# A build-time scheduler that lets transfers queue for one shared bandwidth

## The chip, the cores and the metric

The kernel runs on one core of one Trainium2 chip. The metric is the device time of one execution in microseconds (us). A change of 0.2%, about 2.4 us, is roughly what a measurement of this kernel can tell from no change.

## What is computed

One layer of a hybrid decoder, on 1024 tokens of width 1024, in float32. The mixer has three groups of heads side by side: a short gated convolution (256 columns), a gated DeltaNet (512 columns, 4 heads of 128) and a stick-breaking attention (256 columns, 4 heads of 64).

```python
h = rmsnorm(x, w_norm_mix)
sc_b, sc_c, sc_h, gq, gk, gv, gz, ga, gb, sq, sk, sv = split(h @ w_mix_in)
y_sc = sc_b * causal_dwconv(sc_c * sc_h, w_sconv)
gq, gk, gv = split(silu(causal_dwconv([gq, gk, gv], w_gdn_conv)))
# DeltaNet, in chunks of 64 tokens: decay matrices from the gates,
# a triangular solve with (I + lower(k k^T)), then a scan over the chunks
o = gated_delta_rule_chunked(l2norm(gq), l2norm(gk), gv, g, beta)
y_gdn = rmsnorm(o, w_gdn_norm) * silu(gz)
y_sb = stick_breaking_attention(sq, sk, sv)
x = x + [y_sc, y_gdn, y_sb] @ w_mix_out
gate, val = split(causal_dwconv(rmsnorm(x, w_norm_ffn) @ w_ffn_up, w_ffn_conv))
x = x + (silu(gate) * val) @ w_ffn_down
return rmsnorm(x, w_norm_final)
```

## The kernel before

Every operand of a large product is split into a high and a low part, and a product is three matmuls (high by high, low by high, high by low), which are the lines L316, L318 and L320 for the in-projection and L1310, L1312 and L1314 for the out-projection.

The first half of the program, the *front* (the opening aside), is put in order by a small event simulator, the class `Flow`, that runs while the program is built. Each piece of work is a Python generator, a *process*. It yields a request: an engine with an estimated duration, a buffer to take, or an event to wait for. `Flow.grant` gives each engine to the request with the best class and due time among those that are ready in its model, advances the model's clock, and the process then emits its instructions. So the model's clock decides the order in which each engine's instructions stand in the program, for all five engines; on the chip each engine then runs its own list strictly in that order, and semaphores keep the data right. A model time that is too short or too long makes no wrong result; it puts instructions behind, or ahead of, others.

A transfer is issued on SyncE (SP). In `grant` it holds SP for 60 ns of model time, and the process that asked goes on after a landing time. `sp(kb)` makes it 2000 + 5 ns per KB: 3.28 us for 256 KB, 4.56 us for 512 KB. Each transfer has its landing time for itself, however many are under way. In `prep3` the first three of a block's four loads ask for a landing time of 0, and only the fourth, `sp(256)`, is waited for.

The processes that the prediction speaks of, and their names in the trace:
- `dense` (L537): the in-projection, a column tile `pd3` to `pd25` after the other, 8 steps each; one step is the three products of one pair of row blocks (two instructions each of L316, L318, L320). `pd22` and `pd23`, then `pd24` and `pd25` (which alternate), are the last. Their weights are `w22` and so on.
- `inverse` (L872): the triangular inverses of the DeltaNet chunks on VectorE. 31 pairs of operations on `iv` and `LL`, then three stream transposes (L902 once, L905 twice), which the chain's first products on TensorE, `pw1` and `pw0` (L949), need.
- `prep1`, `prep2`, `prep3`, `prep_at`, `prep_v`: for each of eight blocks of 128 tokens, loads of keys, queries, values and gates from DRAM (`ld<-kscr` and so on, 4 loads of 256 KB) and of a decay matrix (`m<-gscr`, 256 KB; the tile of block 0 is `m20`, of block 1 `m21`); then products on TensorE, `pk` (L1041), `pkq` (L1068), `pq` (L1077), `pv` (L1098), between exponentials on ScalarE (ACT) and elementwise work on VectorE (`kds`, `m`, `ld<-pv`).
- `chain` (L1106): the scan over the chunks with its products `pw`, `py`, `p`, `pco` (L1168) and `pyt` (L1196); the outputs go through DRAM (`yscr`) back to SBUF as `yr`, are split by ACT into `yh` and by VectorE into a low part.
- `mo_mm` (L1286): the out-projection `pmo0` to `pmo7`, with 8 weight tiles `wo0` to `wo7`; `wo0` and `wo1` take the columns that come from the short convolution (`a_sch`), `wo2` to `wo7` the others.

Behind the front the 22 pairs of up-projection column tiles and the down-projection are written out by hand.

Of the kernel before, what the change touches and what calls it, by code (L numbers as in the profile page):

```python
# [70 lines left out]
T_AFTER = dict(PE=230, DVE=60, ACT=60, POOL=60, SP=60)  # L71
T_PIPE = dict(PE=0, DVE=80, ACT=100, POOL=60, SP=0)
T_TABLE = 1280


class Flow:
# [4 lines left out]
    def __init__(self, **tokens):  # L81
        self.now = 0.0
        self.events, self.seq = [], 0
        self.free = dict.fromkeys(("PE", "DVE", "ACT", "POOL", "SP"), 0.0)
        self.want = {e: [] for e in self.free}
        self.tokens, self.queue = dict(tokens), {k: [] for k in tokens}
        self.happened, self.waiting = set(), {}
        self.port = dict(DVE=0.0, POOL=0.0)
        self.table = None

    def at(self, t, f, *args):
        self.seq += 1
        heapq.heappush(self.events, (t, self.seq, f, args))
# [64 lines left out]
    def grant(self, e):  # L158
        q = self.want[e]
        pick = heapq.heappop(q)  # L160
        if e == "ACT" and pick[3] not in (None, self.table):
            same = [r for r in q if r[3] in (None, self.table) and r[0] <= pick[0]]
            if same:
                q.append(pick)
                pick = min(same)
                q.remove(pick)
                heapq.heapify(q)
        _, _, ns, what, proc, cls = pick
        t = self.now
        if e == "ACT" and what not in (None, self.table):  # L170
            ns += T_TABLE
            self.table = what
        land = 0
        if e == "SP":
            ns, land = 60, ns
        elif e == "POOL" or e == "DVE" and what:
            other = "DVE" if e == "POOL" else "POOL"
            t = max(t, self.port[other])
            self.port[e] = t + ns
        self.free[e] = t + ns - T_PIPE[e]  # L180
        back, self.now = self.now, t + ns + land + (0 if what == "more" else T_AFTER[e])
        r = next(proc, None)
        if r is not None:
            self.at(self.now, self.handle, proc, cls, r)
        self.now = back
# [3 lines left out]
def trunk(ctx: ExitStack, tc: tile.TileContext, xT, x, cst, wcm, wsv, wout, wnf, wup, wdn, wfin, out):  # L189
# [24 lines left out]
    def e8(shape, name, dt=F32):  # L214
        return T(shape, dt, "e8", name)
# [7 lines left out]
    def small(shape, name, bufs=1):  # L223
        return T(shape, F32, name, name, bufs=bufs)
# [10 lines left out]
    def tt(eng, out_, a, b, op):  # L235
        eng.tensor_tensor(out_, a, b, op=op)  # L236
# [44 lines left out]
    def ms(name):  # L281
        return pp.tile([P, 512], F32, tag="ms", name=name, bufs=4)
# [105 lines left out]
    def pe(ns, due=None, what=None):  # L388

        return "PE", ns, due, what  # L390

    def act(n, table=None, cls=None):
        return "ACT", T_ACT[0] + T_ACT[1] * n, cls, table

    def dve(n, port=True, per=T_DVE, cls=None):
        return "DVE", per[0] + per[1] * n, cls, port

    def pool(n, cls=None):
        return "POOL", T_POOL[0] + T_POOL[1] * n, cls, None

    def sp(kb, cls=None):
        return "SP", 2000 + 5 * kb, cls, None

    def take(tag, n=1):
        return "take", tag, n

    def wait(*what):
        return "wait", what

    def now(*what):  # L410
        fl.happen(what)
# [385 lines left out]
    def load_blk(dst, scr, n):  # L797
        nc.sync.dma_start(dst, scr[:, :, n * P:(n + 1) * P].rearrange("h p c -> p h c"))

    def v4(t):  # L800
        return t[:, 0:512].rearrange("p (h c) -> p h c", h=GH)

    def load_gf(dst, n, m):

        nc.sync.dma_start(dst, gscr[n * GH:(n + m) * GH, :].rearrange("(o h) c -> o (h c)", o=1).broadcast_to([P, m * GH * P]))
# [5 lines left out]
    def bc(ap, m=P):  # L811
        return ap.unsqueeze(2).broadcast_to([P, GH, m])
# [180 lines left out]
    def prep3(n):  # L993
        s = st[n]
        if n == 0:
            for kind in ("gq", "gv", "gz"):
                for j in range(GH):
                    yield wait(kind, j)
            yield wait("norms", NB - 1)
            yield wait("sb", 1)  # L1000
            yield "ACT", 400, None, "exp"
            nc.scalar.preload_act_table_set("natural_log_exp_and_others")
            nc.scalar.activation(snk, nke, AF.Ln)
            nc.scalar.activation(snk, snk, AF.Exp, scale=0.5)
            nc.scalar.activation(egn, Gc, AF.Exp)
            yield "DVE", 200, None, True
            nc.vector.tensor_scalar(egn, egn, -1.0, None, op0=mul)
        else:
            yield wait("ld", n - 1)
        yield take("e8")  # L1010
        ld = e8([P, 4, GH, P], f"ld{n}")
        kb, qb, vb, zb = (ld[:, i] for i in range(4))
        for dst, scr in ((kb, kscr), (qb, qscr), (vb, vscr)):
            yield "SP", 0, None, None
            load_blk(dst, scr, n)
        yield sp(256)
        load_blk(zb, zscr, n)
        now("ld", n)
        if n > 0:
            yield wait("m2", n - 1)  # L1020
        yield take("e8")
        now("m2", n)
        yield sp(256)
        m2 = e8([P, 4, GH, P], f"m2{n}")
        at, dec, eg, kd = (m2[:, i] for i in range(4))
        load_gf(dec.rearrange("p h c -> p (h c)"), n, 1)
        s.update(kb=kb, qe=qb, kd=kd, vs=vb, at=at, zb=zb, jk=dec, m2=m2)
        now("dec", n)
        fl.spawn(prep_v(n), 3)
        fl.spawn(prep_at(n), 3)  # L1030
        yield act(512, "exp")
        nc.scalar.activation(eg, dec, AF.Exp)
        now("eg", n)
        yield pool(4)
        egl = s["egl"] = small([P, GH], "egl", bufs=3)
        nc.gpsimd.tensor_copy(egl, eg[:, :, P - 1])
        yield take("ms")
        yield pe(4 * 109)
        pk = ms(f"pk{n}")
        for h in range(GH):  # L1040
            nc.tensor.transpose(out=pk[:, h * P:(h + 1) * P], in_=kb[:, h, :], identity=ident)  # L1041
        yield wait("kds", n)
        yield dve(512, False)
        tt(nc.vector, kd, v4(pk), bc(s["kds"]), mul)
        fl.give("ms")
        now("kd", n)
# [45 lines left out]
    def prep_v(n):  # L1092
        s = st[n]
        yield take("ms")
        yield pe(4 * 109)
        pv = ms(f"pv{n}")
        for h in range(GH):
            nc.tensor.transpose(out=pv[:, h * P:(h + 1) * P], in_=s["vs"][:, h, :], identity=ident)  # L1098
        yield dve(512, False)
        tt(nc.vector, s["vs"], v4(pv), bc(snk[:, n, :]), mul)  # L1100
        fl.give("ms")
        now("v2", n)
# [993 lines left out]
```

## Time and profile before

| what | value |
|---|---|
| time, median of 3 runs | 1221.97 us (1221.42 to 1223.99) |
| the profiled execution | 1226.06 us, its span 1224.3 us |
| TensorE (PE) busy | 1191.8 us, 97% of the span |
| weight loads (PEld) | 992.8 us, beside the matmuls |
| VectorE (DVE) busy | 939.8 us, 77% |
| ScalarE (ACT) busy | 646.7 us, 53% |
| GpSimd (POOL) busy | 373.3 us, 30% |
| DMA | 152.76 MB, mean 125 GB/s |

The front ends at about 600 us. A row of a timeline gives the start in the span, the duration, the engine, the line, the operation with output and inputs, a count, and in brackets the idle time before it and what ended it. A row of a waits view gives what waited and for what: total us, times, longest. `PEclk` is the clock granted to TensorE, where 1.00 is the upper level.

### The profile page before, as it was taken

The page shows a single profiled execution, that of the slowest core. Times are in us where ns is not written, and L with a number is a line of the kernel's source. Part 1 is how long each engine was busy: PE and PEld are TensorE (multiplying, and loading weights), DVE is VectorE, ACT ScalarE, POOL GpSimd, SP SyncE. Part 2 cuts the span into 40 slices and gives each one's busy share as a digit, 9 for nine tenths or more (in the row PEclk, how much of TensorE's full clock was granted, in tenths as well). Part 3 has the DMA queues.
Part 4 walks back from the last instruction along what each step waited for, and adds up shares of the span by engine and source line. Part 5 has one row for each costly group of instructions (what it writes and reads, how often), then busy time and mean ns, then how long its engine had stood idle before and what let it go on. Part 6 is the DMA issues. An engine that isn't in the chain of part 4 may idle for free.

```text
span 1224.3 us, 16593 instructions
## 1 busy us (share of the span) xinstructions
PE 1191.8 (97%) x6083; PEld 992.8 (81%) x6083; DVE 939.8 (77%) x1340; ACT 646.7 (53%) x1102; POOL 373.3 (30%) x299
## 2 busy tenths in 40 slices
PE   8999999999999999999999999999999999999997
PEld 6798888888878878888788888888888887888886
DVE  3776779977993557557988988889889878985774
ACT  6766576778323544544655454553545534454554
POOL 3444433433335433000024544234443322001200
PEclk9999999999998989999999999999999999999999
DMA  9111132332271663444123333223333279852314
GB/s 347 53 56 43 54 127 89 106 108 91 87 217 36 178 169 102 140 142 141 60 67 99 128 112 111 82 97 115 116 108 104 69 267 352 300 138 81 99 52 146
DMA packets 87089, 152.76 MB, mean 125 GB/s; under 512 B 6592, under 2 KB 42464, under 8 KB 86752
## 3 DMA queue, kind: packets, MB, share of 16 engines
q1 hardware_dynamic: 86864, 151.59, 38.3%
q8 instruction: 48, 0.79, 0.3%
q14 instruction: 33, 0.27, 0.1%
q10 hardware_dynamic: 144, 0.10, 0.1%
HBM read 110.50 MB, written 41.17 MB: 124 GB/s over the span
## 4 chain that ended last, share of the span: by engine, by line
PE 81%; DVE 5%; DMA 5%; ACT 4%; issue 2%; SPq 1%; POOL 1%; ACTq 0%; DVEq 0%; POOLq 0%
PE pu L1571 19%; PE pz L1571 10%; PE pdx L1739 8%; PE pdzP L1739 7%; PE pd L316 6%; PE pd L318 5%; PE pd L320 5%; PE py L1571 4%; PE pmo L1310 2%; PE pmo L1312 2%; PE pmo L1314 2%; DMA m<-gscr 1%; PE po L690 1%; DMA xs<-x_in 1%; PE pa L668 1%
## 5 line engine op out<-in xcount | busy, mean ns | idle before, releaser
L236 POOL TENSOR_TENSOR ws<-wu 128x512 f32<-128x512 f32 x40 | 62.1, 1573 | 172.4 <-DMA wu<-wup_in 172.4
L236 POOL TENSOR_TENSOR sg<-sg,om 128x511 f32<-128x511 f32 (+3 forms) x64 | 60.7, 958 | 118.0 <-DVE om L653 62.1
L239 DVE SCALAR_TENSOR_TENSOR ua<-uv,ck,ua 128x1023 f32<-128x1023 f32 (+1 forms) x44 | 76.1, 1729 | 7.4 <-ACT ua L233 7.3
L239 DVE SCALAR_TENSOR_TENSOR ua<-ug,ck,ua 128x1023 f32<-128x1023 f32 (+1 forms) x44 | 76.0, 1727 | 0.8
L233 ACT ACTIVATE ua<-ug,ck 128x1024 f32<-128x1024 f32 x22 | 25.4, 1154 | 86.8 <-DVE ug L236 86.8
L1665 ACT ACTIVATE ua<-ua 128x1024 f32<-128x1024 f32 x22 | 23.4, 1062 | 84.8 <-DVE ua L239 84.8
L236 POOL TENSOR_TENSOR x<-x,wfb 128x512 f32<-128x512 f32 x8 | 12.8, 1636 | 126.3 <-ACT y L1755 126.3
L236 DVE TENSOR_TENSOR S<-ws,S 128x512 fp32r<-128x512 f32 x52 | 39.8, 770 | 5.5 <-ACT S L231 4.3
L236 DVE TENSOR_TENSOR at<-pa,at 128x512 fp32r<-128x512 f32 (+3 forms) x48 | 26.1, 549 | 22.6 <-ACT at L231 22.4
L231 ACT ACTIVATE S<-ws 128x512 fp32r<-128x512 f32 x52 | 32.5, 630 | 20.2 <-DVE ws L236 10.4
L1310 PE MATMUL pmo<-wo,yh 128*128 128x512 f32 x128 | 41.4, 404 | 0.0
L231 ACT ACTIVATE at<-pa 128x512 fp32r<-128x512 f32 (+3 forms) x48 | 23.4, 487 | 33.0 <-PE pa L668 31.7
L236 POOL TENSOR_TENSOR A<-wu,A 128x512 fp32r<-128x512 f32 x11 | 15.9, 1449 | 80.4 <-ACT A L231 80.4
L1312 PE MATMUL pmo<-wo,yh 128*128 128x512 f32 x128 | 39.7, 392 | 0.0
L1314 PE MATMUL pmo<-wo,yr 128*128 128x512 f32 x128 | 39.6, 390 | 0.0
L653 DVE TENSOR_TENSOR_SCAN om<-om 128x512 f32<-128x512 f32 (+3 forms) x32 | 33.7, 1066 | 7.0 <-ACT om L644 6.1
L236 DVE TENSOR_TENSOR A<-wu,A 128x512 fp32r<-128x512 f32 x29 | 28.4, 983 | 11.7 <-ACT A L231 11.7
L1571 PE MATMUL py<-fB21h,A 128*128 128x512 f32 x112 | 36.7, 389 | 0.0
L1571 PE MATMUL pz<-fB22h,S 128*128 128x512 f32 x112 | 36.7, 389 | 0.0
L1571 PE MATMUL pu<-fB11h,A 128*128 128x512 f32 x104 | 34.1, 389 | 0.0
L1571 PE MATMUL pu<-fT3h,S 128*128 128x512 f32 x104 | 34.1, 389 | 0.0
L1571 PE MATMUL pu<-fT4h,A 128*128 128x512 f32 x104 | 34.1, 389 | 0.0
(1446 smaller groups left out, 3958.9 us busy)
## 6 DMA issues: line engine op xcount, KB each, us to landing
wu<-wup_in SPq DMA_DIRECT2D x44, 512.0 KB, 3.9
gaP<-gst SPq DMA_DIRECT2D x77, 256.0 KB, 3.2
w<-wcm_in SPq DMA_DIRECT2D x23, 512.0 KB, 3.6
wd<-wdn_in SPq DMA_DIRECT2D x44, 256.0 KB, 5.9
gst<-g SPq DMA_DIRECT2D x12, 512.0 KB, 2.6
gst<-uv SPq DMA_DIRECT2D x10, 512.0 KB, 2.9
xs<-x_in SPq DMA_DIRECT2D x4, 1024.0 KB, 11.4
wor<-wout_in SPq DMA_DIRECT2D x8, 512.0 KB, 3.8
```

Of the source, the lines that this page charges most:

```text
L231: nc.scalar.activation(out_, in_, AF.Copy)
L236: eng.tensor_tensor(out_, a, b, op=op)
L239: nc.vector.scalar_tensor_tensor(out_, a, s, b, op0=op0, op1=op1)
L316: nc.tensor.matmul(ps[th], lhsT=w_h, rhs=xh[k // 2][:, k % 2, th * 512:(th + 1) * 512], start=first, stop=False)
L318: nc.tensor.matmul(ps[th], lhsT=w_h, rhs=xl[k // 2][:, k % 2, th * 512:(th + 1) * 512], start=False, stop=False)
L320: nc.tensor.matmul(ps[th], lhsT=w_l, rhs=xh[k // 2][:, k % 2, th * 512:(th + 1) * 512], start=False, stop=last)
L653: nc.vector.tensor_tensor_scan(om[:, 0:w][:, ::-1], om[:, 0:w][:, ::-1], om[:, 0:w][:, ::-1], init, op0=mul, op1=ALU.bypass)
L1310: nc.tensor.matmul(po[:, c * 512:(c + 1) * 512], lhsT=h, rhs=wh_[:, c * 512:(c + 1) * 512], start=first, stop=False)
L1312: nc.tensor.matmul(po[:, c * 512:(c + 1) * 512], lhsT=h, rhs=wl_[:, c * 512:(c + 1) * 512], start=False, stop=False)
L1314: nc.tensor.matmul(po[:, c * 512:(c + 1) * 512], lhsT=l, rhs=wh_[:, c * 512:(c + 1) * 512], start=False, stop=last)
L1571: nc.tensor.matmul(o, lhsT=w[:, wk], rhs=b[:, k, :], start=first and k + j == 0, stop=k == 3 and j == 2, skip_group_check=not first)
L1739: nc.tensor.matmul(o, lhsT=a[:, tk], rhs=b, start=first and u == 0 and j == 0, stop=u == NU - 1 and j == 2, skip_group_check=not first)
```

## The change

Three lines change the model. `grant` keeps one number, `moved`, the model time at which the transfers so far have been moved. A transfer of `what` KB adds 3.4 ns per KB to it, from the present time or from the end of the transfers ahead, whichever is later. Its process goes on 3 us (`T_LAND`) after that. So 256 KB alone take 3.87 us (before 3.28), 512 KB 4.74 (before 4.56), 64 KB 3.22 (before 2.32), and each transfer that is still queued ahead of one adds its own share, 0.87 us for 256 KB and 1.74 us for 512 KB. In `prep3` the first three loads of a block are not waited for, as before, but now count 256 KB each, so the fourth lands 2.6 us later, and what is issued behind them too.

```diff
--- before.py
+++ after.py
@@ -71,6 +71,8 @@
 T_AFTER = dict(PE=230, DVE=60, ACT=60, POOL=60, SP=60)
 T_PIPE = dict(PE=0, DVE=80, ACT=100, POOL=60, SP=0)
 T_TABLE = 1280
+T_KB = 3.4
+T_LAND = 3000
 
 
 class Flow:
@@ -87,6 +89,7 @@
         self.happened, self.waiting = set(), {}
         self.port = dict(DVE=0.0, POOL=0.0)
         self.table = None
+        self.moved = 0.0
 
     def at(self, t, f, *args):
         self.seq += 1
@@ -172,7 +175,9 @@
             self.table = what
         land = 0
         if e == "SP":
-            ns, land = 60, ns
+
+            self.moved = max(t, self.moved) + T_KB * what
+            ns, land = 60, ns and self.moved - t + ns
         elif e == "POOL" or e == "DVE" and what:
             other = "DVE" if e == "POOL" else "POOL"
             t = max(t, self.port[other])
@@ -399,7 +404,7 @@
         return "POOL", T_POOL[0] + T_POOL[1] * n, cls, None
 
     def sp(kb, cls=None):
-        return "SP", 2000 + 5 * kb, cls, None
+        return "SP", T_LAND, cls, kb
 
     def take(tag, n=1):
         return "take", tag, n
@@ -1011,7 +1016,7 @@
         ld = e8([P, 4, GH, P], f"ld{n}")
         kb, qb, vb, zb = (ld[:, i] for i in range(4))
         for dst, scr in ((kb, kscr), (qb, qscr), (vb, vscr)):
-            yield "SP", 0, None, None
+            yield "SP", 0, None, 256
             load_blk(dst, scr, n)
         yield sp(256)
         load_blk(zb, zscr, n)
```

No engine gains or loses an instruction, except that ACT loads its function tables 35 times where it did 42 times. The order within the front changes from about 225 us to the front's end on every engine; the hand-written part behind it stays nearly as it was. All lines shift by 2 to 5 (L902 is L907, L905 is L910, L949 is L954, L1168 is L1173, L1310 is L1315).

DVE at the end of the inverse, before:

```order
L236 TENSOR_TENSOR iv_2833<-LL_2082 128x60
L239 SCALAR_TENSOR_TENSOR m20_3163<-m20_3163,Gc_370,maskadd_74 128x128 x4
L236 TENSOR_TENSOR LL_2082<-LL_2082,iv_2833 128x2x30
L236 TENSOR_TENSOR ld0_3126<-pv0_3201,snk_374 128x512
L236 TENSOR_TENSOR m20_3163<-pk0_3209,kds_3188 128x512
L236 TENSOR_TENSOR iv_2833<-LL_2082 128x31
L236 TENSOR_TENSOR LL_2082<-LL_2082,iv_2833 128x31
L236 TENSOR_TENSOR kds_3244<-m21_3193,Gc_370 128x4
L239 SCALAR_TENSOR_TENSOR m20_3163<-pkq0_3228,br2_373,m20_3163 128x128 x4
L236 TENSOR_TENSOR kds_3244<-kds_3244,br2_373 128x4
L239 SCALAR_TENSOR_TENSOR m21_3193<-m21_3193,Gc_370,maskadd_74 128x128 x4
L902 STREAM_TRANSPOSE LL_2082<-LL_2082 128x32x32
```

And now:

```order
L241 TENSOR_TENSOR iv_2850<-LL_2082 128x60
L241 TENSOR_TENSOR p_scc0_3165<-pd20_3063,rb_111 128x1024
L241 TENSOR_TENSOR LL_2082<-LL_2082,iv_2850 128x2x30
L241 TENSOR_TENSOR iv_2850<-LL_2082 128x31
L241 TENSOR_TENSOR LL_2082<-LL_2082,iv_2850 128x31
L907 STREAM_TRANSPOSE LL_2082<-LL_2082 128x32x32
L241 TENSOR_TENSOR kds_3211<-m20_3183,Gc_370 128x4
L910 STREAM_TRANSPOSE LL_2082<-xi0_3193 128x16x32
L241 TENSOR_TENSOR kds_3211<-kds_3211,br2_373 128x4
L241 TENSOR_TENSOR ld0_3129<-pv0_3213,snk_374 128x512
L910 STREAM_TRANSPOSE LL_2082<-xi1_3194 128x16x32
```

The operations on block 0's tiles (`m20`, `ld0`) and block 1's (`m21`, whose decay matrix is a DMA load) stood among the last steps of the inverse and ahead of its first transpose; now they stand behind the first transpose or behind all three.

PE at the first products that need the inverse, `pw1` and `pw0`, before:

```order
L316 MATMUL pd23_3432<-xh2_105,w23h_3341 128x512 x2
L318 MATMUL pd23_3432<-xl2_106,w23h_3341 128x512 x2
L320 MATMUL pd23_3432<-xh2_105,w23l_3352 128x512 x2
L949 MATMUL pw1_3491<-LL_2082,U0_1673 32x32 x8
L316 MATMUL pd23_3432<-xh2_105,w23h_3341 128x512 x2
L318 MATMUL pd23_3432<-xl2_106,w23h_3341 128x512 x2
L320 MATMUL pd23_3432<-xh2_105,w23l_3352 128x512 x2
L949 MATMUL pw0_3508<-LL_2082,U0_1673 32x32 x8
L316 MATMUL pd23_3432<-xh3_107,w23h_3341 128x512 x2
```

And now:

```order
L321 MATMUL pd22_3274<-xh1_103,w22h_3157 128x512 x2
L323 MATMUL pd22_3274<-xl1_104,w22h_3157 128x512 x2
L325 MATMUL pd22_3274<-xh1_103,w22l_3167 128x512 x2
L954 MATMUL pw1_3353<-LL_2082,U0_1673 32x32 x8
L954 MATMUL pw0_3363<-LL_2082,U0_1673 32x32 x8
L321 MATMUL pd22_3274<-xh2_105,w22h_3157 128x512 x2
L323 MATMUL pd22_3274<-xl2_106,w22h_3157 128x512 x2
L325 MATMUL pd22_3274<-xh2_105,w22l_3167 128x512 x2
L1046 MATMUL pk1_3384<-ident_70,ld1_3182 128x128 x4
L1073 MATMUL pkq1_3389<-ld1_3182 128x128 x4
L967 MATMUL py0_3395<-Tt0_3237,w10_3381 32x32 x8
```

They stood behind 5 of 8 steps of `pd23` and are now behind 4 steps of `pd22`. Nine steps of `pd22` and `pd23`, and seven groups of block products (`pk1`, `pkq1`, `pv2`, `pk2`, `pq1`, `pkq2`, `pq2`), which were ahead of them, stand behind them now.

SP at the load of `w25`, the last weight tile of the in-projection, before:

```order
L798 DMA ld2_3191<-kscr_88 128x4x128
L805 DMA m21_3193<-gscr_92 128x512
L798 DMA ld2_3191<-qscr_89 128x4x128
L798 DMA ld2_3191<-vscr_90 128x4x128
L798 DMA ld2_3191<-zscr_91 128x4x128
L798 DMA ld3_3250<-kscr_88 128x4x128
L805 DMA m22_3252<-gscr_92 128x512
L798 DMA ld3_3250<-qscr_89 128x4x128
L798 DMA ld3_3250<-vscr_90 128x4x128
L798 DMA ld3_3250<-zscr_91 128x4x128
L519 DMA w25_3368<-wcm_in 128x1024
```

And now:

```order
L803 DMA ld2_3258<-kscr_88 128x4x128
L810 DMA m21_3260<-gscr_92 128x512
L803 DMA ld2_3258<-qscr_89 128x4x128
L803 DMA ld2_3258<-vscr_90 128x4x128
L803 DMA ld2_3258<-zscr_91 128x4x128
L524 DMA w25_3308<-wcm_in 128x1024
L803 DMA ld3_3340<-kscr_88 128x4x128
L810 DMA m22_3342<-gscr_92 128x512
```

The load of `w25` stood behind the loads of block 3 and of `m22`; now it is ahead of them. It needs the buffer of `w23`, which comes free when POOL has made the low part `w23l`. On POOL that operation stood ahead of the copies out of the finished inverse (`Tt0`, `t641`, `t640`); now the first of these copies are ahead of it. And on ACT the exponential of `m22` now stands ahead of the copies `t640` and `Tt0` from the chain's product `py0`, for which the next product, `pw20`, waits.

Three more places in words. `pg7`, the last product on PE that the inverse takes its inputs from, stands four dense steps later in PE's list, while DVE's list has five rows less up to the inverse's last step. The chain used to have the steps of `pd23` to `pd25` and of `pmo0` and `pmo1` between its products; now it has those of `pd22` to `pd25` and is over, `pco7` included, when `pmo0` begins. From `p12` to `pw24` its products now follow each other without a dense step between (`p12`, `pw23`, `pkq3`, `p22`, `py23`, `pw4`, `p42`, `pq3`, `py4`, `pco2`, `p13`, `pv4`, `pw24`), where before two steps lay between `p12` and `p13`. And in `pmo0` now `wo2` to `wo7` come first, six steps, with `pyt7` among them, then `wo0` and `wo1`, which need the 128 KB of `yr0` that hold the short convolution's output: `a_sch` on DVE from the last two column tiles, to DRAM (`yscr`), back as `yr0`, through ACT (`yh`) and DVE.

## Rows read from the trace of the kernel before

**Rows 1.** Page, part 1: busy time, share of the span, instructions.
```profile
PE 1191.8 (97%) x6083; PEld 992.8 (81%) x6083; DVE 939.8 (77%) x1340; ACT 646.7 (53%) x1102; POOL 373.3 (30%) x299
```
**Rows 2.** Windows: stretch, length, busy of PE, PEld, DVE, ACT, POOL (instructions), PEclk, DMA share, GB/s.
```profile
225.00:340.00 115.00, 112.81 (x578) 94.19 (x577) 96.13 (x225) 73.09 (x116) 37.85 (x28) 1.00 0.30 99
340.00:352.00 12.00, 11.31 (x63) 9.06 (x61) 10.39 (x29) 3.29 (x8) 3.07 (x4) 1.00 1.13 314
352.00:360.00 8.00, 5.71 (x25) 4.75 (x26) 8.00 (x17) 2.10 (x5) 1.30 (x2) 0.79 0.64 170
...
387.00:397.00 10.00, 9.46 (x79) 8.25 (x79) 1.16 (x1) 3.84 (x9) 5.79 (x4) 0.66 0.18 54
397.00:425.00 28.00, 27.19 (x253) 23.38 (x253) 15.94 (x34) 15.62 (x35) 13.54 (x17) 1.00 0.54 157
425.00:429.00 4.00, 3.25 (x23) 2.64 (x22) 2.63 (x4) 2.07 (x5) 2.21 (x5) 1.00 0.99 308
...
446.00:455.00 9.00, 6.15 (x34) 4.90 (x33) 4.25 (x11) 2.91 (x10) 1.08 (x2) 0.62 0.49 131
...
508.00:512.00 4.00, 2.80 (x15) 2.36 (x15) 2.64 (x4) 1.86 (x5) 0.00 (x0) 1.00 0.09 24
```
**Rows 3.** Waits of PE, 340 to 600 us: total us, times, longest.
```profile
PE pk L1041 <- ACT t L231: 2.8, 1, 2.8
PE pv L1098 <- ACT m L1079: 2.0, 1, 2.0
PE pyt L1196 <- DVE on L236: 1.7, 2, 1.2
```
**Rows 4.** DMA issues of the whole span: count, KB each, median us to landing.
```profile
ld<-kscr SPq DMA_DIRECT2D x8, 256.0 KB, 5.8
...
m<-gscr SPq DMA_DIRECT2D x8, 256.0 KB, 5.2
...
yscr<-a_sch SPq DMA_DIRECT2D x2, 512.0 KB, 4.4
...
yr<-yscr SPq DMA_DIRECT2D x1, 128.0 KB, 5.5
```
**Rows 5.** Waits of all engines, 240 to 600 us: ACT for the decay matrix.
```profile
ACT m L1032 <- DMA m<-gscr: 17.1, 6, 4.5
```
**Rows 6.** Timeline of DVE, end of the inverse.
```profile
346.92 1.14 DVE L239 SCALAR_TENSOR_TENSOR m<-m,Gc,maskadd 128x128 f32<-128x128 f32 x4
...
348.10 0.69 DVE L236 TENSOR_TENSOR ld<-pv,snk 128x512 f32<-128x512 f32 x1
...
349.52 0.19 DVE L236 TENSOR_TENSOR LL<-LL,iv 128x31 f32<-128x31 f32 x1
351.01 0.16 DVE L236 TENSOR_TENSOR kds<-m,Gc 128x4 f32<-128x4 f32 x1 [1.30 <-DMA m<-gscr]
...
354.11 2.08 DVE L902 STREAM_TRANSPOSE LL<-LL 128x1024 f32<-128x1024 f32 x1
...
364.02 1.14 DVE L905 STREAM_TRANSPOSE LL<-xi 128x512 f32<-128x512 f32 x1
```
**Rows 7.** Timeline of PE: two starts of a dense step, a block group, the first `pw`.
```profile
319.05 0.62 PE L316 MATMUL pd<-xh,w19h 128*128 128x512 f32 x2
...
320.41 0.62 PE L316 MATMUL pd<-xh,w19h 128*128 128x512 f32 x2
...
358.67 0.84 PE L1041 MATMUL pk<-ident,ld 128*128 128x128 f32 x4
...
380.37 0.59 PE L949 MATMUL pw<-LL,U 32*32 32x32 f32 x16
```
**Rows 8.** Timeline of SP: the load of `w25`.
```profile
364.10 0.35 SPq L519 DMA_DIRECT2D w<-wcm_in  x1
```
**Rows 9.** Timeline of POOL: the low part `w23l`.
```profile
361.68 2.40 POOL L236 TENSOR_TENSOR w23l<-w,w23h 128x1024 fp32r<-128x1024 f32 x1 [5.52 <-ACT w23h L231]
```
**Rows 10.** Timeline of DVE: the short convolution's output.
```profile
458.71 1.21 DVE L236 TENSOR_TENSOR a_sch<-pd,a_sch 128x1024 f32<-128x1024 f32 x1
```

## The prediction

> **What bounds the kernel now.** The page's first part comes first: PE is busy 97% of the span [rows 1], so no instruction that stays can be made shorter by this change, and all there is to win is PE's idle time and the time in which its clock is low. Then the windows, for the front alone, since the order changes only there. Between 225 and 340 us PE is idle 2.19 us of 115 at clock 1.00. Between 340 and 512 us the stretches shown are idle 0.69, 2.29, 0.54, 0.81, 0.75, 2.85 and 1.20 us, 9.1 us in all, and in three of them the granted clock is 0.79, 0.66 and 0.62 (1.00 is 2.4 GHz, half of it 1.2 GHz) [rows 2]. What a low clock costs I take as (1 - clock) x PE's busy time: 0.21 x 5.71 = 1.2, 0.34 x 9.46 = 3.2, 0.38 x 6.15 = 2.3, together 6.7 us. So 15.8 us is the ceiling of what a better order can give back.
>
> Next, who ends these idle times. PE's longest waits are for ACT: `pk` 2.8 us and `pv` 2.0 us [rows 3]. ACT itself waited 17.1 us in six waits for the decay matrices, `m<-gscr` [rows 5], and on the chip such a load lands in 5.2 us, one of `ld` in 5.8 [rows 4], where the model of before has them land in 3.28. ACT and DVE run their lists in order, so a block operation placed too early holds everything behind it. DVE shows it: the inverse's last step is at 349.52, then comes a wait for `m<-gscr`, the first transpose at 354.11 and the last only at 364.02 [rows 6].
>
> **The change, part by part.** No instruction goes but seven table loads on ACT, which is not the bound; the terms are stalls of PE.
>
> *A, 340 to 360 us* (idle 0.69 + 2.29, clock 1.2) [rows 2]: block products wait here for ACT. They now stand behind `pw1`, and block 0's DVE work behind the inverse. Taken whole, 4.2 us, if nothing takes their place. That depends on two times. The inverse: its loop ended at 349.52 + 0.19; without 1.14 + 0.69 us of block 0's work and another operation as long as the second [rows 6] it ends at 347.2. Behind it are 2.08 and twice 1.14 us of transposes, one 0.69 and two 0.16 between: ready at 352.6, where it was 365.2. PE: it reached `pw1` at 380.37; it now comes there nine steps of 1.36 us (320.41 - 319.05) earlier, 12.2 us; seven block groups earlier (0.84 us at clock 0.79 [rows 2, 7], so 0.66 each), 4.6 us; and 4.2 us earlier for A: at 359.4. That leaves 6.8 us of slack, so no wait.
>
> *B, 387 to 397 us* (0.54 idle, 3.2 clock): the chain's first products, small and with few steps between. They now get the steps of `pd22` and `pd23`, but `p12` to `pw24` become such a place instead. Between 0 and 3.7 us; I take half, 1.8.
>
> *C, 397 to 425 us* (0.81) I leave where it is. *D, 425 to 429 us*: 0.75, behind a late decay matrix; taken. *E, 446 to 455 us* (2.85 idle, 2.3 clock): `pk` behind ACT, which again waited for a decay matrix [rows 3, 5]. The new model gives such a load 3.87 us and 0.87 more for each of its kind ahead, 6.5 for the fourth of a bunch, against 5.2 to 5.8 measured, so the exponentials should now stand where the data is there. Between 0 and 5.2; I take 4.2. *F, 508 to 512 us*: `pyt7` for the last output, 1.20 idle [rows 2]; it waits again, but with fewer table loads ahead. Between 0 and 1.2; I take 0.6.
>
> Gains: 4.2 + 1.8 + 0.75 + 4.2 + 0.6 = 11.55 us.
>
> Losses. *The tail*: behind the chain's end PE has `pco7` (two groups, 1.3 us), six steps (8.2) and `pyt7` (0.66), 10.2 us, before it needs `yr0`'s last part. That part's way is `a_sch`, 1.21 [rows 10], 4.4 to DRAM and 5.5 back [rows 4], and two operations on ACT and DVE for which 0.69 each is the nearest row: 12.5 us. The rest, 2.3 us, is a wait if all of it begins at the last step, and 0.4 if the first of the two `a_sch` halves is out earlier and the transfers take 1 us less each; I take 1.9. Before, chain products covered this. *Stalls of the new order* that I can't see: between 0 and the 9.1 us of now. The nearest row is the front's earlier part, where the same model drives the same engines: 2.19 in 115 us [rows 2], so 3.3 in 172.
>
> Sum: 11.55 - 1.9 - 3.3 = 6.35 us. Against the profiled execution's 1226.06 that is 1219.7; it stands 4.1 us over the median of the runs, and against the median of 1221.97 it is 1215.6. I say 1215.5. The best case is all gains, 15.0, less 0.4: 1207.4.
>
> A rule speaks against this. The rows say that a 256 KB load lands in 5.2 to 5.8 us, later than either model has it when it is alone [rows 4]. The Trainium skill, "DMA: Bandwidth & Descriptors", section "Anatomy of one DMA — SWDGE (gpsimd) path", fits a transfer as about 2.0 us plus its bytes at 436 GB/s, each by itself; that is 2.6 us for 256 KB, an estimate from the page, nearer to the old model than to the new. By it terms A to E would be nothing and the sum about zero. The trace disagrees for these loads, which come in bunches (DMA share 1.13 in the window from 340 us); the page's path is another engine's.
>
> **The rivals.**
>
> *1. The landing times were not the fault.* If loads mostly land as the old model said, and the waits come from work on ACT and DVE that is longer than its cost there, a longer landing time only moves work later, and stalls form again at other places: about 9 us idle as now, 1222. For it: most of PE's waits name ACT, not a DMA, in the row [rows 3]. Against it: the measured 5.2 and 5.8 [rows 4] and ACT's 17.1 us [rows 5]. The page's fit named above points this way. 0.06.
>
> *2. Part of the gain is given back at the chain's start.* The inverse is 2 to 6 us later than 352.6, by part of the 5.4 us that rival 3 names; the slack at `pw1` hides that, but the wait at `pw20` that rival 3 prices grows by 1.2 to 5.2 us with a low clock of up to 2.3 on top: 1216.8 to 1223.1, 1221 in the middle of its upper part. 0.11.
>
> *3. Slower: the load of `w25` holds up the chain.* It now stands ahead of `m22`'s load on SP, and waits for `w23l` on POOL (2.40 us [rows 9]), which is behind the first copies out of the inverse. And ACT's exponential of `m22` stands ahead of the copies that `pw20` needs. With the inverse ready at 352.6, about 2 us of copies (no row; as much as `w23l`) and 2.4 for `w23l`, `w25` goes at 357, not at 364.10 [rows 8]; `m22` goes some 1 us behind, lands 5.2 later at 363.2, and ACT is past it at about 364.5. PE is at `pw20` two steps and four or five groups behind `pw1`, at 365.3. So 0.8 us of slack: each further us of a late inverse costs PE one, and E shows what comes on top, a low clock for 2.3 us. If the inverse is as late as before, 12.6 us later, PE stalls 11.8 + 2.3 = 14.1 us, and the time is 1215.6 + 14.1 = 1229.7. It ends over 1224.4 when stall and clock take back 8.8 us, that is from 7.3 us late on (7.3 - 0.8 + 2.3): an inverse ready past 360. For it: `pg7`, an input of the inverse, stands four steps (5.4 us) later in PE's list, and my 352.6 can be out by a few us besides. Against it: DVE's list up to the inverse's last step is shorter now. 0.13.
>
> **How the numbers follow.** My forecast, that the terms hold within their bounds, 0.70. The single cases spread from 1207.4 (all gains) to 1219 (gains halved or unseen stalls doubled). About 0.2%, 2.4 us, is what a measurement of this kernel can tell from no change, so "same" is 1219.6 to 1224.4. Faster: 0.70. Same: rivals 1 and 2, less 0.01 for what of rival 1 ends above, 0.16. Slower: rival 3 and that 0.01, 0.14. The range goes from all gains to where "slower" begins and so leaves out 0.14 above and next to nothing below: 1207.5 to 1224.
>
> **What would show it.** Right: in the changed kernel's windows PE's clock stays near 1.00 from 340 to 500 us and the idle there falls from 9.1 to about 4; the three transposes start between 346 and 353 us; `pw1` is at about 359 with no wait; PE's waits of `pk` and `pv` for ACT are gone; ACT's waits for `m<-gscr` are well below 17.1 us; `pco7` ends before `pmo0` begins, and one wait of 1 to 3 us for `yr` or `yh` stands at `pmo0`'s seventh step. Wrong: a wait of PE at `pw1` for the transposes or at `pw20` for ACT, with `w25` leaving past 362 us (rival 3); ACT's waits for `m<-gscr` as long as before with PE idle at other block products (rival 1); a wait over 5 us at the tail; or a low clock between `p12` and `pw24` as deep as B's, which would take back its 3.7 us.

## The result and the profile after

The changed kernel takes 1206.65 us (median of 5 runs, 1206.0 to 1207.4) against 1223.14 for the kernel before, run beside it (5 runs, 1221.42 to 1228.38). The ratio is 0.9868, interval 0.985 to 0.9885: 14 to 18 us less, where 6.5 had been forecast, and 0.85 us below the stated range. Two executions among all those below took far longer than the others of their kernel (6777 us in e11, 1691 us in e15) and are left out of its median.

Where the time went is read from one mark that both programs have, the first product of the up-projection, behind the front. The row gives the first and the last start. Before:

```profile
L1571 PE MATMUL pu<-fB11h,A x104: 389/389/389, 583.3 to 985.4; 128*128 128x512 f32 x104
```

And after:

```profile
L1576 PE MATMUL pu<-fB11h,A x104: 389/389/389, 564.8 to 966.9; 128*128 128x512 f32 x104
```

Both are 18.5 us earlier: the gain was won ahead of this mark, and the stretch from its first to its last start takes as long as before. The page's first part, of after:

```profile
PE 1183.1 (98%) x6083; PEld 988.1 (82%) x6083; DVE 948.1 (79%) x1340; ACT 637.2 (53%) x1095; POOL 374.9 (31%) x299
```

PE's busy time fell by 8.7 us with the same 6083 instructions [rows 1], so a low clock had cost about 8.7 us; the rest is idle time. How a late matrix led to both shows in the longest wait of before, on ACT and on PE:

```profile
448.17 0.63 ACT L1032 ACTIVATE m<-m 128x512 f32<-128x512 f32 x1 [3.61 <-DMA m<-gscr]
```

```profile
449.35 1.11 PE L1041 MATMUL pk<-ident,ld 128*128 128x128 f32 x4 [2.85 <-ACT t L231]
```

ACT stood 3.61 us at the exponential of a matrix that had not landed; the copy `t` behind it in ACT's list came late, and PE waited 2.85 us for that copy. The granted clock of this stretch was 0.62 [rows 2].

The windows of after, with the columns of [rows 2]:

```profile
225.00:340.00 115.00, 115.00 (x593) 97.24 (x592) 104.04 (x231) 70.78 (x114) 41.03 (x29) 1.00 0.34 107
340.00:352.00 12.00, 12.00 (x67) 10.15 (x65) 11.67 (x26) 3.44 (x7) 3.13 (x9) 1.00 0.82 237
352.00:360.00 8.00, 7.57 (x89) 6.19 (x88) 7.79 (x10) 3.93 (x10) 6.90 (x8) 1.00 0.58 169
360.00:387.00 27.00, 26.69 (x249) 22.98 (x249) 17.20 (x33) 12.92 (x35) 13.02 (x18) 1.00 0.21 54
387.00:397.00 10.00, 10.00 (x103) 8.36 (x101) 6.41 (x19) 5.44 (x17) 2.44 (x7) 1.00 0.57 172
397.00:425.00 28.00, 28.00 (x270) 24.51 (x270) 17.75 (x40) 15.25 (x39) 14.65 (x24) 1.00 0.57 151
425.00:446.00 21.00, 20.61 (x205) 18.05 (x203) 15.83 (x36) 11.96 (x28) 10.46 (x6) 1.00 0.56 170
446.00:455.00 9.00, 8.69 (x77) 8.07 (x78) 7.69 (x21) 3.12 (x8) 3.80 (x3) 1.00 0.18 60
455.00:470.00 15.00, 14.55 (x99) 13.14 (x99) 12.10 (x18) 6.90 (x13) 3.65 (x2) 1.00 0.29 98
```

The clock is 1.00 in every row. Between 340 us and the front's end PE is idle 1.9 us (0.43 + 0.31 + 0.39 + 0.31 + 0.45), where it was 9.1; between 225 and 340 it is not idle at all, where it was 2.19 [rows 2]. Together 7.2 + 2.2 + 8.7 = 18.1 of the 18.5 us. PE's waits of after from 340 to 600 us, without one of 0.8 us that lies behind the front and was there before too, and ACT's for the decay matrix from 240 to 600:

```profile
...
PE py L990 <- DVE S L241: 0.6, 1, 0.6
PE pyt L1201 <- DVE on L241: 0.4, 1, 0.4
PE pv L1103 <- DVE m L241: 0.4, 1, 0.4
PE p L1150 <- ACT vn L236: 0.3, 1, 0.3
```

```profile
ACT m L1037 <- DMA m<-gscr: 0.2, 1, 0.2
```

ACT's 17.1 us [rows 5] have become 0.2, while the loads take about as long as before. The DMA issues of after between 225 and 600 us:

```profile
ld<-kscr SPq DMA_DIRECT2D x8, 256.0 KB, 5.2
...
ld<-zscr SPq DMA_DIRECT2D x8, 256.0 KB, 6.5
m<-gscr SPq DMA_DIRECT2D x8, 256.0 KB, 5.5
```

Before, it was 5.8 for `ld<-kscr`, 6.0 for `ld<-zscr`, the fourth load of a block, and 5.2 for `m<-gscr`. So these loads did not get faster. What needs a load now stands where the load is there.

The inverse and what hangs on it, of after: DVE's last step and its first and last transpose; `pw1` and `pw20` on PE; the load of `w25` on SP; ACT's exponential of `m22`.

```profile
342.88 0.19 DVE L241 TENSOR_TENSOR LL<-LL,iv 128x31 f32<-128x31 f32 x1
343.11 2.25 DVE L907 STREAM_TRANSPOSE LL<-LL 128x1024 f32<-128x1024 f32 x1
...
347.06 1.09 DVE L910 STREAM_TRANSPOSE LL<-xi 128x512 f32<-128x512 f32 x1
```

```profile
354.92 0.89 PE L954 MATMUL pw<-LL,U 32*32 32x32 f32 x32
...
362.54 0.65 PE L982 MATMUL pw<-t,U 64*64 64x64 f32 x8
```

```profile
353.99 0.34 SPq L524 DMA_DIRECT2D w<-wcm_in  x1
```

```profile
360.25 0.62 ACT L1037 ACTIVATE m<-m 128x512 f32<-128x512 f32 x1
```

The inverse is ready at 348.2 (forecast 352.6), PE comes to `pw1` at 354.9 (359.4), `w25` leaves at 354.0 (357); neither `pw1` nor `pw20` waits.

The tail, of after: on SP the stores of `a_sch` and the loads of `yr`, on ACT `yh`, on DVE `a_sch` and the low part of `yr`, on PE the first step with `wo0`.

```profile
469.62 1.45 SPq L453 DMA_DIRECT2D yscr<-a_sch  x2
...
475.37 0.89 SPq L1269 DMA_DIRECT2D yr<-yscr  x2
```

```profile
478.79 0.42 ACT L236 ACTIVATE yh<-yr 128x256 fp32r<-128x256 f32 x1 [4.17 <-DMA yr<-yscr]
```

```profile
468.38 2.34 DVE L241 TENSOR_TENSOR a_sch<-pd,a_sch 128x1024 f32<-128x1024 f32 x2
...
479.24 0.43 DVE L241 TENSOR_TENSOR yr<-yr,yh 128x256 fp32r<-128x256 f32 x1 [0.32 <-ACT yh L236]
```

```profile
479.36 0.62 PE L1315 MATMUL pmo<-wo,yh 128*128 128x512 f32 x2
...
480.29 0.63 PE L1319 MATMUL pmo<-wo,yr 128*128 128x512 f32 x2
```

From `a_sch`'s start to the end of `yr`'s low part it is 11.3 us, and PE gets to `wo0` as it ends. `yh` is there at 479.21, 0.15 us ahead of the product that takes it.

### The profile page after: what moved, and what is told of

It is laid out like the page before. It is cut to its first block, busy times and chain, and to the rows that moved or that the text cites. A ratio compares the mean times of both kernels' runs of the same rounds, so it can differ in the third digit from the quotient of the medians.

```text
span 1205.4 us, 16599 instructions
## 1 busy us (share of the span) xinstructions
PE 1183.1 (98%) x6083; PEld 988.1 (82%) x6083; DVE 948.1 (79%) x1340; ACT 637.2 (53%) x1095; POOL 374.9 (31%) x299
## 4 chain that ended last, share of the span: by engine, by line
PE 85%; DVE 5%; DMA 3%; ACT 3%; issue 2%; POOL 1%; SPq 0%; DVEq 0%; ACTq 0%; POOLq 0%
PE pu L1576 19%; PE pz L1576 10%; PE pdx L1744 8%; PE pdzP L1744 7%; PE pd L321 6%; PE pd L323 6%; PE pd L325 6%; PE py L1576 4%; PE pmo L1317 2%; PE pmo L1315 2%; PE pmo L1319 2%; PE po L695 1%; DMA xs<-x_in 1%; PE pa L673 1%; DMA xT<-xT_in 1%
## 5 line engine op out<-in xcount | busy, mean ns | idle before, releaser
L1315 PE MATMUL pmo<-wo,yh 128*128 128x512 f32 x128 | 40.3, 396 | 0.0
L241 DVE TENSOR_TENSOR ws<-ws,wu 128x512 f32<-128x512 f32 x22 | 25.9, 1178 | 10.7 <-POOL ws L241 10.7
L1576 PE MATMUL pu<-fT2h,S 128*128 128x512 f32 x104 | 34.1, 389 | 0.0
```

The source lines that it names most:

```text
L1315: nc.tensor.matmul(po[:, c * 512:(c + 1) * 512], lhsT=h, rhs=wh_[:, c * 512:(c + 1) * 512], start=first, stop=False)
L1576: nc.tensor.matmul(o, lhsT=w[:, wk], rhs=b[:, k, :], start=first and k + j == 0, stop=k == 3 and j == 2, skip_group_check=not first)
```

## The experiments

The runs e1 to e16 test these theories. **L**: what pays is a landing time in the model as long as the real one, for the loads of the block preparation above all. **M**: of these, the wait of ACT and DVE for decay matrices. **Q**: the queue itself. **P**: only the block work ahead of the inverse hurt. **S**: the order of before was a bad draw and any other is better. **T** came later: what is lost or hidden in the tail, at `pmo0`. Times are medians; the kernel before ran beside each group, at 1222.7, 1222.8, 1221.4 and 1223.8 us.

**e1, the inverse first, old landing times.**

```diff
-    fl.spawn(inverse(), 3)
+    fl.spawn(inverse(), 2.5)
```

> The kernel before, with its old landing times; only the inverse's process has a better class (2.5 instead of 3) than the block preparation. In the order block 0's five operations stay ahead of the inverse's end, with the wait for m21's load, but the three transposes then follow each other nearly at once and pw1 stands 8 dense steps earlier. Theory L (landing times that are too short put work ahead of its data, all over the front): gains A in part, 2 to 4 us, E and B stay: 1218 to 1221. Theory P (only the block work ahead of the inverse hurt, and the rest followed from it): most of the 16 us, 1207 to 1211. Theory S (the order of before was a bad draw, any other is better): anywhere between 1207 and 1218.

1223.76 us, ratio 1.0008 (0.9988 to 1.0029): nothing, where L had expected 2 to 4 us. DVE, and ACT's waits for the decay matrix:

```profile
352.46 0.16 DVE L236 TENSOR_TENSOR kds<-m,Gc 128x4 f32<-128x4 f32 x1 [2.96 <-DMA m<-gscr]
...
353.58 2.14 DVE L902 STREAM_TRANSPOSE LL<-LL 128x1024 f32<-128x1024 f32 x1
```

```profile
ACT m L1032 <- DMA m<-gscr: 18.8, 7, 4.4
```

The transposes follow each other now and end at 358.4, not 365.2, and `pw1` stands eight steps earlier, yet nothing is won: the waits for decay matrices are all there. P's gain is not there, and S in its plain form, that any other order is better, falls. P is not quite tested by this run, since one of these waits still stands ahead of the transposes; e2 and e7 below do it.

**e2, the new costs without the queue.**

```diff
-            self.moved = max(t, self.moved) + T_KB * what
-            ns, land = 60, ns and self.moved - t + ns
+            ns, land = 60, ns and T_KB * what + ns
```

> The changed kernel with the new costs (3 us and 3.4 ns per KB) for each transfer alone, without the queue: 3.87 us for 256 KB. Theory L says the queue is needed for the bunched loads, which land in 5.2 to 6 us, so a good part is lost: 1212 to 1217. Theory Q (the queue alone is what pays) says no gain: 1220 to 1223. Theory S says 1207 to 1218. If a single longer time is enough: 1206 to 1209.

1222.82 us, 1.0008 (0.9995 to 1.002): no gain, as Q had it and not L. 3.87 us is too short: ACT still waits 14.7 us for `m<-gscr` and DVE 6.0. And a second loss appears, at the first steps of `pmo0`:

```profile
PE pmo L1314 <- ACT yh L235: 6.0, 1, 6.0
```

Here the transposes end at 341.5 us, and no wait for a matrix stands ahead of them on DVE; in e7 they end at 347.8, likewise. With the inverse as early as in the change, neither run has its gain, so P is refuted.

**e3, two longer landing times, no queue.** In the kernel before, for the fourth load of a block and for its decay matrix, both:

```diff
-        yield sp(256)
+        yield "SP", 5900, None, None
```

> The kernel before, and only the two landing times in the block preparation (the fourth load and the decay matrix) are 5.9 us instead of 3.28; no queue, all other transfers as before. Theory L: these loads were the fault, nearly the whole gain: 1207 to 1211. Theory Q: 1215 to 1222, since weights and loads still don't queue. Theory P: the inverse is ahead of the block work here, so as L. Theory S: 1207 to 1218.

1206.91 us, 0.9888 (0.9869 to 0.9907): the whole gain, from two numbers and without the queue. The fewer table loads of ACT are not the cause either: e1 and e5, which win nothing, have as many as e3 (ACT x1097), and e7 as many as the change (x1095). The front's earlier part stays as before:

```profile
225.00:340.00 115.00, 112.82 (x576) 94.12 (x575) 96.30 (x223) 72.23 (x114) 37.53 (x28) 1.00 0.33 105
```

**e4, the queue with the old cost of one transfer** (`T_KB = 5.0`, `T_LAND = 2000`).

> The changed kernel with the old cost of a single transfer (2 us and 5 ns per KB, 3.28 us for 256 KB) but with the queue, the three loads counted. Theory Q: the whole gain, 1206 to 1209. Theory L: the bunched loads get 5.8 us and more, so most of the gain too, 1207 to 1211. If it is the longer fixed time of 3 us: 1214 to 1222. Theory S: 1207 to 1218.

1210.93 us, 0.9921 (0.9899 to 0.9942): most of the gain. ACT waits 0.5 us for `m<-gscr`; 3.0 us are lost at `pmo0`, for `yh` and `a_sch`.

**e5 and e6, one of e3's two numbers each:** only the decay matrix's in e5, only the fourth load's in e6.

> The kernel before; of the two landing times in the block preparation only the decay matrix's (m2, L1032's exponential waits for it) is 5.9 us instead of 3.28, the fourth load's stays. If the exponential on ACT that stands ahead of its data is the whole fault (theory M): as the longer times for both, 1206 to 1210, and ACT's waits for m<-gscr gone. If the load zb, on which the start of the next block's loads hangs in the model, matters as well: 1211 to 1218.

> The counterpart: only the fourth load's landing time is 5.9 us, the decay matrix's is 3.28. Theory M: ACT still waits for m<-gscr, 10 us and more, and little is gained, 1217 to 1223. If it is the time by which the block work as a whole comes later in the model: 1207 to 1212, and ACT's waits are gone all the same.

e5: 1223.48 us, 1.0004 (0.9982 to 1.0026). e6: 1216.84 us, 0.9948 (0.9927 to 0.9968). In e5 the waits of ACT and DVE for the matrices are down to 5.7 us, as M has it, and still nothing is won. PE's waits there:

```profile
PE pmo L1310 <- ACT yh L231: 5.8, 1, 5.8
PE pq L1077 <- DVE m L239: 2.5, 1, 2.5
```

M alone is refuted: PE's wait in the tail, which before did not have, takes the place of those that are gone. In e6 10.8 us of the waits are left, and three fifths of the gain are missing. e5's time lies outside both ranges that had been expected, e6's just below M's.

**e7, one part undone:** in the changed kernel the decay matrix lands after 3.28 us, outside the queue.

```diff
-            self.moved = max(t, self.moved) + T_KB * what
-            ns, land = 60, ns and self.moved - t + ns
+            if what is None:
+                ns, land = 60, ns
+            else:
+                self.moved = max(t, self.moved) + T_KB * what
+                ns, land = 60, ns and self.moved - t + ns
...
-        yield sp(256)
+        yield "SP", 3280, None, None
```

> The changed kernel with one part undone: the decay matrix's transfer lands after 3.28 us again, neither queued nor counted in the queue; all others as changed. Theory M: the waits of ACT for m<-gscr come back, 8 to 17 us, and with them half or more of the gain is lost, 1214 to 1222. If the queue of the four loads before it is enough, since it moves the decay matrix's issue too: 1206 to 1210.

1220.49 us, 0.9974 (0.9956 to 0.9992): more than four fifths of the gain gone, with 13.3 us of waits of ACT and 12.2 of DVE for `m<-gscr`. What stands ahead of PE's longest wait of this run shows on DVE, POOL and PE:

```profile
406.41 0.16 DVE L244 TENSOR_TENSOR kds<-m,Gc 128x4 f32<-128x4 f32 x1 [0.89 <-DMA m<-gscr]
...
408.71 5.94 DVE L247 SCALAR_TENSOR_TENSOR m<-m,Gc,maskadd 128x128 f32<-128x128 f32 x4
```

```profile
408.50 1.04 POOL L244 TENSOR_TENSOR sx<-S,egl 128x512 f32<-128x512 f32 x1
409.50 2.39 POOL L244 TENSOR_TENSOR w25l<-w,w25h 128x1024 fp32r<-128x1024 f32 x1
411.86 2.38 POOL L244 TENSOR_TENSOR p_sch<-p_sch,p_scc 128x1024 f32<-128x1024 f32 x1
```

```profile
416.00 2.08 PE L1076 MATMUL pkq<-ld 128*128 128x128 f32 x8 [5.14 <-ACT w L239]
```

The late matrix is not itself PE's wait: DVE stood only 0.89 us for it. Four decay operations behind it, which took 1.14 us before [rows 6], take 5.94, beside three operations of POOL; ACT's copy behind them and PE follow. That without the 0.89 us these operations would have missed POOL's is argued here, not shown.

**e8, no queue, every transfer longer** (`4600 + 3.4 * kb` in the kernel before, 5.47 us for 256 KB).

> The kernel before, no queue; every transfer lands after 4.6 us and 3.4 ns per KB (256 KB 5.47 us, 512 KB 6.34, 64 KB 4.82), about what the rows say for the loads of the block preparation. Theory L: no queue is needed, only a time that is long enough: 1206 to 1210. If too long a time for weights and outputs costs something: 1210 to 1215. If the queue has a part of its own: 1212 to 1219.

1205.71 us, 0.9864 (0.9826 to 0.9901): as the change, without its queue. With e3, this refutes Q: a plain longer time does what the queue does. PE is not idle between 225 and 340 us here, unlike e3: so the 2.2 us there hang on the other transfers' times.

**e9 to e12, how long is right:** e3's two numbers at 4.5 and at 7.5 us, the change with `T_LAND` 4000, and e8 with 6600 instead of 4600.

> As the kernel with 5.9 us for the two landing times of the block preparation (1206.9), but with 4.5 us, below what the rows show for these loads (5.2 to 6.1). Theory L (a time as long as the real one is needed, and enough): ACT still waits for m<-gscr some us, and part of the gain is lost: 1210 to 1219. Theory S (any other order would do, no trend): anywhere, as likely below 1210 as above.

> The same with 7.5 us, longer than these loads take. Theory L: no wait for m<-gscr is left, work merely comes later in the model than it could: 1205 to 1211. Theory S: anywhere up to 1222.

> The changed kernel with a fixed time of 4 us instead of 3, the queue as it is. Theory L: as the change, since it errs on the long side: 1204 to 1209. If the change's constants are a lucky pair (theory S): 1210 to 1220.

> The kernel before, no queue, every transfer 6.6 us and 3.4 ns per KB (256 KB 7.47 us), about two us longer than the run in which all were 5.47 and which took 1205.7. Theory L with no price for too long a time: 1205 to 1209. If weights and the products' inputs that come late in the model leave PE without the right work at hand (the inverse is reached 8 steps later): 1209 to 1217. A wait of ACT for m<-gscr: none in either case.

1213.19, 1216.37, 1212.32 and 1210.12 us (ratios 0.9925, 0.9951, 0.9916, 0.9899). e9 is as L said, with ACT waiting 11.0 us for the matrices. The other three hardly wait for them (0.3 us at most) and lose elsewhere, against L's expectation for e10 and e11. e11 falls where a lucky pair of constants had been expected to fall, e12 where too long a time has a price. e11:

```profile
PE pmo L1315 <- ACT yh L236: 4.7, 1, 4.7
```

e12 waits 3.3 us in `pmo` too, for `yh` and `yr`; e10 1.6 for `yh`, 1.7 for a weight tile `wo` and 1.6 at `pkq`. That is theory T. In the orders of e2, e5, e10 and e11, 8, 5, 8 and 3 steps of `pd24` and `pd25` stand behind `pco7`, just ahead of `pmo0`, so `a_sch` ends with them; in the change, e3 and e8 none do. In e12 none do either, so its wait has another cause, which no run shows.

**e13, the tail's cover taken away:** `pmo0` takes `wo0` first.

```diff
-        ks = (2, 3, 4, 5, 6, 7, 0, 1) if n == 0 else range(KT)
+        ks = range(KT)
```

> The changed kernel; only pmo0 takes its weight tiles in the order wo0 to wo7, so that the first two, which need the short convolution's output from DRAM, have nothing ahead of them but pco7. The transfers are the same. Theory T (the tail's way through DRAM, 11 us from a_sch to yr0 in the changed kernel's trace, is there as forecast, and only the six steps ahead hide it): PE waits 8 to 9 us at the start of pmo0, and the clock is low behind it for some 2 to 3 us: 1216 to 1219. If yr0 comes much sooner when nothing else is queued: 1207 to 1211.

1217.64 us, 11.0 over the change. The profiled execution was the fastest of its eight, 1214.23, 6.8 over that of the change, and PE is idle 6.8 us longer in it. The window of the tail, and PE's waits:

```profile
470.00:480.00 10.00, 3.93 (x11) 2.95 (x12) 5.41 (x8) 1.98 (x5) 2.48 (x1) 0.67 1.03 320
```

```profile
PE pyt L1201 <- DVE on L241: 4.9, 2, 4.5
PE pmo L1315 <- ACT yh L236: 2.3, 1, 2.3
```

The way through DRAM is there, and only the six steps hide it: PE waits 4.5 us for the input of `pyt7`, runs it, and waits 2.3 us more for `yh`, less than the 8 to 9 us of T; the clock falls, as T said.

**e14, e15, e16:** `T_LAND` 2500 and 2800, and the three loads uncounted (`256` set to `0` in `prep3`).

> The changed kernel with a fixed time of 2.5 us instead of 3 (256 KB 3.37 us alone, 5.97 for the fourth load of a block). In its order all steps of the in-projection are over before pco7, as in the change. Theory L with T: no tail wait, few waits for m<-gscr: 1206 to 1211. Theory S: 1206 to 1220.

> The same with 2.8 us, still nearer to the change; but in its order three steps of the in-projection come behind pco7, right ahead of pmo0, as in the run with 4 us, which had a wait of 4.7 us for yh in pmo0. Theory T: that wait is there, 3 to 6 us, and the time is 1210 to 1215, above the run with 2.5 us. If nearness of the constants decides: 1206 to 1208.

> The changed kernel with one part undone: the three loads of a block that are not waited for no longer count in the queue. The fourth load alone then lands after 3.87 us, and the decay matrix after 3.87 and what happens to be queued. Theory M (the wait of ACT and DVE for decay matrices that the model has there too early): their waits for m<-gscr are back, 8 us or more in sum, and 1213 to 1222. If the fixed 3 us and the queue of the other transfers do it: 1206 to 1209.

1211.10 us (0.9885, 0.9856 to 0.9914), 1213.95 (0.9907, 0.9871 to 0.9942) and 1209.99 (0.9877, 0.9847 to 0.9908). e14 has no wait in `pmo`, as expected, but 15.0 us of the waits for matrices where few had been expected, and 1.8 us of idle time between 225 and 340 us. e15 has PE's wait for `yh`, 3.9 us, and 0.7 for `a_sch`; it is the slower of the two although its constant is nearer to the change, as T said from its order. In e16 10.2 us of the waits for the matrices are back but only 3.3 us are lost, less than M had and more than the other case had. So such waits have no fixed price.

All but e13 side by side: waits of ACT and DVE for `m<-gscr` from 225 to 600 us and PE's waits in `pmo`, both from the profiled execution, and the median.

| kernel | waits for matrices | waits in `pmo` | us |
|---|---|---|---|
| before | 26.8 | 0 | 1222.7 |
| e1 | 27.8 | 0.6 | 1223.8 |
| e7 | 25.5 | 0 | 1220.5 |
| e2 | 20.7 | 6.0 | 1222.8 |
| e14 | 15.0 | 0 | 1211.1 |
| e9 | 13.1 | 0 | 1213.2 |
| e6 | 10.8 | 0 | 1216.8 |
| e16 | 10.2 | 0 | 1210.0 |
| e5 | 5.7 | 5.8 | 1223.5 |
| e15 | 2.3 | 4.6 | 1214.0 |
| e11 | 0.3 | 4.7 | 1212.3 |
| e10 | 0.2 | 3.3 | 1216.4 |
| e12 | 0 | 3.3 | 1210.1 |
| e4 | 0.5 | 3.0 | 1210.9 |
| e3 | 2.3 | 0 | 1206.9 |
| the change | 1.9 | 0 | 1206.7 |
| e8 | 1.2 | 0 | 1205.7 |

Only the three with little of either are below 1209. Neither column gives the time by itself. And the change is not where it is by right landing times alone: with `T_LAND` at 2500, 2800 and 4000 instead of 3000 it loses 4.5, 7.3 and 5.7 us of its 16.5, in e15 and e11 with hardly a wait for a matrix left. That the order of 3000 hides the tail as well is in part luck.

## Why the prediction was wrong

The direction and the mechanism were right: model times that were too short, ACT and DVE held by loads that were not there, stalls and a low clock on PE behind them. The queue itself was not needed for it (e3, e8). The size was wrong, by several terms, all on the cautious side.

- *Stalls of the new order, 3.3 us*, is the step that failed first. I took the idle rate of 225 to 340 us as what this scheduler always leaves. But that idle time, too, goes with the model's landing times: 2.2 us with the old times for the other transfers (before, e1, e3, e5, e6, e9, e10), 1.8 and 0.7 with times near the old ones (e14, e4), none in the change and 0.0 to 0.3 with longer ones for all (e2, e7, e8, e11, e12, e15, e16). So there was a gain of 2.2, and all idle time left behind 340 us is 1.9. That is 3.6 us of the difference. The 1.9 is partly luck: e12, e15 and e11 have 5.0 to 6.9 us there.
- *The clock.* I multiplied what was missing in it by PE's busy time and got 6.7 us. PE was idle mostly before the clock fell and busy while it was low, so the window's length is the better factor: 0.21 x 8 + 0.34 x 10 + 0.38 x 9 = 8.5, against the 8.7 by which the busy time fell. That is 2.0 us.
- *B, half taken.* The new place from `p12` to `pw24` (392.8 to 403.7 us) has no idle time and keeps clock 1.00, and the whole of B was won: 1.9 us. Of E and F, taken in part, 1.6 more, and C's 0.8, which I had left where it is; what stays of them is in the 1.9 us above.
- *The tail, 1.9 us*: no wait. The mechanism is real (e13: 11 us without its cover), but the 128 KB of `yr0` landed in 3.4 us where I had 5.5 [rows 4], and the way took 11.3 us, not 12.5. It is covered with 0.15 us to spare.

Together 11.8 us, and with the sum's 6.35 that is 18.1 of the 18.5 us between the profiled executions at the mark. The medians differ by 16.5, since the profiled execution of before stood 2.9 us above its median and that of the change 0.75. The ceiling that I had worked out first, 15.8 us, was nearer than the sum from which I had taken guesses off.

Of the rivals, 1 is refuted by e3 and e8. 2 did not occur: `pg7` was 5.7 us later (285.9, was 280.2), but DVE's list made that up and the inverse was 4.4 us earlier than I said. 3 did not occur either: `w25` left at 354.0. The rule of the Trainium skill that the prediction named ("DMA: Bandwidth & Descriptors", section "Anatomy of one DMA — SWDGE (gpsimd) path"; 2.6 us for 256 KB, an estimate from the page) had the sum at zero. The trace disagrees for these loads, whose medians are 5.2 to 6.5 us in both kernels. e2, with 3.87 us, gained nothing: 20.7 us of the waits for matrices were left, and the tail cost 6.0 us more.

What is not settled is which step of their orders makes e6 and e10 as slow as they are. Their stalls are there: e10 is idle 2.2 us between 225 and 340 us and 5.8 behind, and its clock costs some 3.6, an estimate from 20 us windows; e6 has 2.2, 5.7 and some 6.8. But they are spread over several waits, the longest 2.4 us, and no run took one of them away.

## What to carry to other kernels

In a build-time scheduler an estimate that is too short can do more harm than its size: it puts an operation ahead of its data on an engine that runs in order, and all that is behind it waits too. Compare each modelled time with the landing that the trace shows for that kind of transfer, in the bunch in which it runs, before looking for a better policy: two numbers set to 5.9 us, where the fourth load of a block took 6.0 and the decay matrix 5.2, did what the queue does; 4.5 lost 6 us of it, and 7.5 lost 9, so too long a time was no safe side here. A single good time does not show that a model is right either: with three other values of `T_LAND` the kernel was 4 to 7 us slower. And when one stall goes, look at the end of the stretch: here orders that left the in-projection's last steps behind the chain exposed 2 to 6 us of a way through DRAM that had been hidden.

## What the runs showed of the hardware

The first observation is on TensorE's clock. In the kernel before, it fell in two kinds of places. One is idle time (about 353 to 355 and 446.5 to 449 us). The other had hardly any: some 2 us of 32x32 and 64x64 products with two short gaps between. PE's timeline and single microseconds of the windows, of before:

```profile
388.47 0.47 PE L985 MATMUL py<-Tt,t 64*64 64x64 f32 x5 [0.30 <-ACT t L231]
...
389.64 1.89 PE L1129 MATMUL p<-ld,Tt 128*128 128x128 f32 x8 [0.24 <-ACT Tt L233]
```

```profile
388.00:389.00 1.00, 0.70 (x19) 0.62 (x15) 0.16 (x1) 0.94 (x4) 1.00 (x1) 1.00 0.00 0
389.00:390.00 1.00, 0.76 (x11) 0.62 (x8) 0.00 (x0) 0.95 (x3) 1.00 (x1) 0.94 0.06 16
390.00:391.00 1.00, 1.00 (x7) 1.00 (x6) 0.00 (x0) 0.00 (x0) 1.00 (x2) 0.50 0.00 0
...
396.00:397.00 1.00, 1.00 (x7) 1.00 (x6) 0.00 (x0) 0.00 (x0) 0.00 (x0) 0.65 0.00 0
```

The clock was at its lower level from about 389.9 to 396.7 us, and PE was busy all that time. In the change the clock stays at 1.00 where such products have dense steps or block products between them, and it stays also from 392.8 to 403.7 us, where small products follow each other without a dense step but without a gap. So products without dense steps do not lower the clock by themselves; whether the gaps did, or the kind of products around them, no run separates. The clock also goes with the spread between runs: the kernel before has 1218.3 us at a mean clock of 0.996 and 1229.8 at 0.989, the change 1206.0 to 1207.4, all near 0.998.

The second is the 5.94 us of e7's four decay operations on DVE, beside three operations of POOL that ended at 409.54, 411.89 and 414.24 us: three of the four on DVE end just behind these, at about 409.6, 412.0 and 414.3. The Trainium skill, "SBUF — State Buffer", section "SBUF: two separate sides", says that the two engines share a port pair, which the one that starts first holds for its whole instruction while the other stands still, for VectorE when its operation has two inputs in SBUF; the trace agrees, with 1.14 us become 5.94.
